# One accumulating DMA issued behind two sums of w1 instead of ahead of them, in a gated MLP kernel

## The chip, the core and the metric

The kernel runs on one core of a Trainium2 chip. The core has five engines that run side by side, each with its own queue in program order: TensorE (PE, matrix products), VectorE (DVE), ScalarE (ACT), GpSimd (POOL) and SyncE (SP). DMAs are issued from the queues of SyncE, GpSimd and ScalarE and all share the core's 16 DMA engines. An engine waits on semaphores for the data of others; whatever stands behind a waiting instruction on the same engine waits too. The metric is the time on the device in microseconds (us).

## What is computed

```python
# x (16, 256, 512), w1 (512, 4096), w2 (2048, 512), float32
h = x @ w1
gate, value = np.split(h, 2, axis=-1)
h = np.maximum(gate, 0) * value
return (h @ w2).astype(np.float32)
```

With the first two axes of x joined there are 4096 rows.

## The kernel before

The rows are worked in four sets of 1024 (`SET`, loop over `s`). Both products use a scheme of the Strassen and Winograd kind: operands are split in two by two, and seven products (P1 to P7) of sums of the parts stand in for eight. So each operand needs sums besides its own parts: T1 to T4 of the weights (`TURNS`), S1 to S4 of x and of g (`SUMS`). All operands are float16, sums on TensorE's side are kept in PSUM in float32.

**First product.** The hidden dimension is cut in 16 blocks `jb` of 128. A block takes seven slots of two matmuls of 128x512 (`Block`, L195 on, matmuls at L202). In the loop P1, P5, P2, P6 and P3, P7, P4 of neighbouring blocks are interleaved (`SLOT`, `PERIOD`). In set 0, blocks 0 to 3 are done in the ordinary way (`Plain`). ScalarE and VectorE turn the results into g = relu(gate) * value (L209 to L241); g is written as float16.

**Second product.** `mm2_stream` (matmuls at L286, 128x256) yields one matmul at a time. It starts while the last blocks of the first product end, and its last `TAIL` steps run into the next set. Its operands are w2's parts, the sums of w2 and the sums of g (L275). In set 0 the order of its steps is P1 and P2 for three row blocks, then P5, P6, P3, P7, P4: P5 needs T1 and S1, P6 needs T2 and S2, P3 needs S4, P7 needs T3 and S3, P4 needs T4.

**Weights.** w1 comes in six chunks (`CHUNKS`), cast to float16 by GpSimd's DMAs (L352). Its sums T1 to T4 are made on GpSimd, one chunk after the other (L160, `w1_one`), each reading what the two parts hold or what an earlier sum has made: T1 from B12 and B11, T2 from B22 and T1, T3 from B22 and B12, T4 from B21 and T2, all added. The last chunk (blocks 12 to 15) is one instruction of 128x1024 for each T. The sums of w2 are made by DMAs alone: SyncE copies parts of w2 to where T1, T2 with T3, and T4 will be (L536), then GpSimd issues accumulating DMAs, which add a source to what stands at the destination (L163, `add_w2`). T3 and T2 are the two halves of one tile, `v_12`, which one copy fills; the profile calls its tile `v`, and the tiles of T1 and T4 `v_T`. The T3 add needs that copy. The T2 add reads T1, so it needs the T1 add to have landed. The T4 add reads T2.

**x.** `cast_x(1)` (L359, a DMA of GpSimd) writes set 1 of x to DRAM as float16. SyncE reads it back transposed (L388). VectorE makes its sums (L451).

**What sets the order.** The scheduling is manual: each engine runs its instructions in the order in which the program text emits them. On GpSimd, around the change, that is: w1 sums of chunks 1 to 4; the T1 and T2 sums of the last chunk (start 40.30 and 42.50); the T1 add of w2 (44.57); the T3 add (50.08); the T3 and T4 sums of the last chunk (50.66, 52.75); the T2 add (54.81); the cast of x (55.39); four sums of g, two for S1 and two for S3 (from 55.95); the T4 add (64.28); one more sum of g for S1 (64.90). VectorE then makes the remaining sums of g of set 0 (L574 to L579): a quarter of S1 (128x1024), S2 in two halves, S4 in two halves, half of S3.

Of the kernel before, what the change touches and what calls it, by code (L numbers as in the profile page):

```python
# [29 lines left out]
@with_exitstack  # L30
def kernel(ctx: ExitStack, tc: tile.TileContext, x, w1, w2, out):

    nc = tc.nc
    x2 = x.flatten_outer_dims()
    out2 = out.flatten_outer_dims()  # L40
    flagpool = ctx.enter_context(tc.tile_pool(name="flagpool", bufs=1))
    flag = flagpool.tile([1, 1], dt.int32, name="flag")
    with ExitStack() as fast:
        unfit = fast_way(fast, tc, x2, w1, w2, out2, flag)
    with tc.If(unfit > 0, label="general"):
        with ExitStack() as general:
            general_way(general, tc, x2, w1, w2, out2)
# [52 lines left out]
def fast_way(ctx, tc, x2, w1, w2, out2, flag):  # L100
# [54 lines left out]
    def w1_ops(eng, jb, n):  # L155
        for t in TURNS:
            w1_one(eng, jb, n, *t)

    def w1_one(eng, jb, n, m, a, b, o):
        eng.tensor_tensor(W(m, jb, n), W(a, jb, n), W(b, jb, n), op=o)  # L160

    def add_w2(m, v):
        nc.gpsimd.dma_start(out=V[m], in_=V[v], accum_op=ADD)  # L163
# [12 lines left out]
    def x_tiles():  # L176
        o = {f"A{h}": xpool.tile([P, 4, TH], F16, name=f"x_A{h}") for h in (1, 2)}
        for h in (1, 2):
            for k in (1, 2):
                o[f"A{h}{k}"] = o[f"A{h}"][:, 2 * k - 2:2 * k]  # L180
        for n in ("S1", "S2", "S3", "S4"):
            o[n] = xpool.tile([P, 2, TH], F16, name=f"x_{n}")
        return o
# [88 lines left out]
    def g_sum(eng, go, n, h0, h1):  # L272
        for m, i0, i1, op in SUMS:
            if m == n:
                eng.tensor_tensor(go[n][:, h0:h1], go[i0][:, h0:h1], go[i1][:, h0:h1], op=op)  # L275
# [69 lines left out]
    def advance(stream, n):  # L345
        for _ in range(n):
            if stream is None or next(stream, 0) == 0:
                return
# [5 lines left out]
    def fetch_w2(i):  # L354
        ks, n = slice(i // 2 * NHC, i // 2 * NHC + NHC), i % 2
        nc.gpsimd.dma_start(out=w2_h[n][:, ks], in_=w2_v[:, ks, n * HALF:(n + 1) * HALF])  # L356

    def cast_x(s):
        nc.gpsimd.dma_start(out=x16[s], in_=x2[s * SET:(s + 1) * SET, :])  # L359

    def g_tiles():
        g = gpool.tile([P, NJ, SET], F16, name="g")
        gs = {n: gpool.tile([P, NHC, TH], F16, name=f"g_{n}") for n in ("S1", "S2", "S3", "S4")}
        return g, g_ops(g, gs)
# [21 lines left out]
    def turn_by_dma(s, o, h):  # L386
        for k in range(2):
            nc.sync.dma_start_transpose(out=o[f"A{h + 1}{k + 1}"], in_=x16[s][h * TH:(h + 1) * TH, k * 256:k * 256 + 256])  # L388
# [7 lines left out]
    def fetch_rows(s, q):  # L396
        rows[s, q] = xpool.tile([P, 2, D], F16, name=f"xn{q % 2}")
        nc.sync.dma_start(out=rows[s, q], in_=x16[s][q * 256:(q + 1) * 256].rearrange("(b p) d -> p b d", p=P))
# [50 lines left out]
    def x_sum(o):  # L449
        n, i0, i1, op = sums.pop(0)  # L450
        nc.vector.tensor_tensor(o[n], o[i0], o[i1], op=op)  # L451
# [64 lines left out]
    for s in range(NS):  # L516
        if s:
            g, go = g_tiles()
        first = NPLAIN if s == 0 else 0
        blocks = {jb: Block(xo, g, jb) for jb in range(first, NJ)}  # L520
        if s == 0:
            blocks[first] = lead
        plan = {jb * PERIOD + at: (jb, n) for jb in blocks for n, at in SLOT.items() if (s, jb, n) != (0, first, "P1")}
        last = NJ * PERIOD
        stream = mm2_stream(s, go)
        if s == 0:
            w1_ops(nc.gpsimd, 4, 2)
            fetch_w2(0)
            fetch_w2(1)
            w1_ops(nc.gpsimd, 6, 2)  # L530
            fetch_w2(2)
            fetch_w2(3)
            w1_ops(nc.gpsimd, 8, 2)
            w1_ops(nc.gpsimd, 10, 2)
            for to, v in ((V["T1"], V["B11"]), (v_12, w2_h[1]), (V["T4"], V["B21"])):
                nc.sync.dma_start(out=to, in_=v)  # L536
            for t in TURNS:
                w1_one(nc.gpsimd, 12, 4, *t)
                if t[0] == "T2":
                    add_w2("T1", "B12")  # L540
                    add_w2("T3", "B22")
            add_w2("T2", "T1")
            cast_x(1)
        for at in range(first * PERIOD, last + PERIOD):
            if at in plan:
                jb, n = plan[at]
                if n == "P1" and s and jb in (4, 8):
                    fetch_rows(s, 1 + jb // 4)
                if n == "P2" and s == 0 and jb in (11, 13, 15):
                    h = jb - 11  # L550
                    if h == 4:
                        add_w2("T4", "T2")
                    for m in ("S1", "S3")[:2 - h // 4]:
                        g_sum(nc.gpsimd, go, m, h, h + 2)
                getattr(blocks[jb], n)()
                ended = jb - (n == "P7") if n == "P7" or (n, jb) == ("P4", NJ - 1) else -1
                if ended in blocks:
                    blocks[ended].finish()
                if n == "P5":
                    for f in LOOKS.get((s, jb), ()):  # L560
                        f()
                if ended >= 0 and s:
                    if ended < NHC:
                        g_sum(nc.gpsimd, go, "S3", ended, ended + 1)
                        if s == 1 and ended in (1, 4):
                            cast_x(2 + ended // 4)
                    elif ended < NJ - BY_DVE:
                        for m in ("S1", "S2", "S4"):
                            g_sum(nc.gpsimd, go, m, ended - NHC, ended - NHC + 1)
            elif at >= last:  # L570
                advance(stream, 4)
            else:
                advance(prev, 4)
        if s == 0:  # L574
            g_sum(nc.vector, go, "S1", 6, 8)
            for m in ("S2", "S4"):
                for h in (0, NHC // 2):
                    g_sum(nc.vector, go, m, h, h + NHC // 2)
            g_sum(nc.vector, go, "S3", NHC // 2, NHC)  # L579
        else:  # L580
            for m in ("S1", "S2", "S4"):
                g_sum(nc.vector, go, m, NHC - BY_DVE, NHC)
        done = 20
        if s + 1 < NS:
            xo = x_tiles()
            for h in range(2):
                turn_by_dma(s + 1, xo, h)
            for q in range(2):
                fetch_rows(s + 1, q)
            advance(stream, 100)  # L590
            sums = list(SUMS)
            for _ in SUMS:
                x_sum(xo)
            if s == 0:
                w1_ops(nc.vector, 0, 2)
                w1_ops(nc.vector, 2, 2)
            advance(stream, MM2 - TAIL - 100 - done)
        else:
            advance(stream, MM2)
        prev = stream  # L600
# [29 lines left out]
```

## Time and profile before

| | us |
|---|---|
| median of 9 runs (lowest to highest) | 313.31 (311.46 to 313.77) |
| the profiled execution, its own time | 314.05 |
| its span, first to last instruction | 312.2 |
| TensorE matmul busy in the span | 302.1 |
| VectorE, ScalarE, GpSimd busy | 217.7, 188.7, 147.2 |
| mean granted TensorE clock | 0.996 |

The profile is of one execution. Busy times count matmuls up to modelled ends. A line of a timeline gives start, duration, engine, line of the kernel, operation, output and input tiles, shapes, and in brackets the engine's idle time in front of it and what ended that. A recorded start of a GpSimd instruction can lie ahead of the end of the one before it; ends follow one another. "DMA to landing" counts from the recorded start of the issue to the last byte's semaphore.

The stretch that the change touches runs from 44 to 74 us, where set 0 ends its first product and starts its second. The DMAs of w2's sums in it, by issue and landing:

| DMA | issued at | to landing |
|---|---|---|
| copy into T2 and T3 (`v_12`, 1024 KB), SyncE | 43.06 | 6.4 |
| T1 add (512 KB), GpSimd | 44.57 | 8.6 |
| T3 add (512 KB), GpSimd | 50.08 | 5.5 |
| T2 add (512 KB), GpSimd | 54.81 | 5.8 |
| cast of x, set 1 (1024 KB), GpSimd | 55.39 | 10.1 |
| T4 add (512 KB), GpSimd | 64.28 | 6.3 |

### The profile page before, as it was taken

To read this page: it belongs to the slowest core of one execution; us is meant where nothing else is said; L and a number is where in the kernel's file an instruction comes from. 1 tells how busy PE (TensorE), PEld (TensorE's weight loads), DVE (VectorE), ACT (ScalarE), POOL (GpSimd) and SP (SyncE) were. 2 spreads that over 40 slices of the span, in tenths; PEclk is the share of its full clock that TensorE was granted. 3 is DMA by queue.
4 is the path that set the end of the run, shared out by engine and by line. 5 is a ranking of instruction groups with operands and counts; after the bars stand their busy time and mean duration, and the time that the engine had idled before them with its cause. 6 is when DMAs were issued, how large, how long until landed. Compare 5 with 4: busy or idle time off the path is not lost.

```text
span 312.2 us, 5081 instructions
## 1 busy us (share of the span) xinstructions
PE 302.1 (97%) x1859; PEld 181.6 (58%) x1859; DVE 217.7 (70%) x330; ACT 188.7 (60%) x450; POOL 147.2 (47%) x135
## 2 busy tenths in 40 slices
PE   7999998998999999999999999999999999999993
PEld 4554443477864444468874444458885444448882
DVE  1377887898638888885428888886525888888311
ACT  3357765646766676748847676655857667673230
POOL 5779985970003346992001424995000434898000
PEclk9999999999999999999999999999999999999998
DMA  7999978969331770036321110028411101000113
GB/s 248 202 202 204 226 191 209 173 110 202 138 122 34 138 163 5 1 70 151 119 101 37 34 34 2 0 44 138 158 70 67 34 3 33 0 2 0 69 73 133
DMA packets 33449, 30.74 MB, mean 98 GB/s; under 512 B 13872, under 2 KB 27952, under 8 KB 33200
## 3 DMA queue, kind: packets, MB, share of 16 engines
q0 software_dynamic: 10704, 11.54, 22.9%
q1 hardware_dynamic: 22576, 18.75, 20.8%
q8 instruction: 15, 0.25, 0.3%
q10 hardware_dynamic: 144, 0.13, 0.1%
q14 instruction: 10, 0.08, 0.1%
HBM read 24.12 MB, written 11.53 MB: 114 GB/s over the span
## 4 chain that ended last, share of the span: by engine, by line
PE 78%; DMA 10%; POOL 6%; issue 2%; DVE 1%; ACT 0%; SPq 0%; DVEq 0%; POOLq 0%
PE Y L202 21%; PE X L202 14%; PE W L202 14%; PE Y L286 13%; PE W L286 8%; PE X L286 8%; DMA w<-in_w_dram 4%; POOL wt L160 4%; DMA wr<-in_w_dram 3%; DMA v<-w 2%; DVE g_S L275 1%; DMA g_S<-in_x_dram 1%; POOL w L356 1%; POOL wr L352 1%; POOL g_S L414 0%
## 5 line engine op out<-in xcount | busy, mean ns | idle before, releaser
L275 POOL TENSOR_TENSOR g_S<-g 128x512 f16<-128x512 f16 (+1 forms) x47 | 60.5, 1331 | 126.0 <-DVE g L241 124.0
L202 PEld LDWEIGHTS <-wt 128*128 128x128 f16 x480 | 46.8, 98 | 57.1 <-POOL wt L160 2.3
L202 PE MATMUL Y<-x_S,wt 128*128 128x512 f16 x240 | 71.4, 379 | 1.1 <-POOL wt L160 1.1
L202 PE MATMUL X<-x_A,wr 128*128 128x512 f16 x240 | 71.4, 379 | 0.0
L202 PEld LDWEIGHTS <-wr 128*128 128x128 f16 x360 | 35.2, 98 | 40.7 <-issue 0.2
L229 DVE SCALAR_TENSOR_TENSOR cc<-W,pu 128x512 f32<-128x512 f32 x60 | 41.5, 692 | 23.6 <-ACT pu L223 23.6
L209 ACT COPY Y<-X 128x512 f32<-128x512 f32 x60 | 34.2, 571 | 37.8 <-PE X L202 37.4
L286 PEld LDWEIGHTS <-g_S 128*128 128x128 f16 x512 | 49.7, 98 | 7.5 <-DVE g_S L275 1.6
L235 DVE SCALAR_TENSOR_TENSOR cc<-Y,pu 128x512 f32<-128x512 f32 x60 | 41.5, 692 | 7.9 <-PE Y L202 2.0
L223 ACT ACTIVATE pu<-Y 128x512 f32<-128x512 f32 x60 | 35.8, 597 | 15.6 <-PE Y L202 15.6
L230 DVE SCALAR_TENSOR_TENSOR g<-X,cc 128x512 f16<-128x512 f32 x60 | 41.5, 692 | 2.3
L286 PEld LDWEIGHTS <-g 128*128 128x128 f16 x384 | 37.6, 98 | 8.2
L241 DVE SCALAR_TENSOR_TENSOR g<-Y,cc 128x512 f16<-128x512 f32 x60 | 40.9, 682 | 1.8 <-PE Y L202 1.8
L216 ACT ACTIVATE pu<-W 128x512 f32<-128x512 f32 x60 | 36.2, 603 | 0.3 <-PE W L202 0.3
L202 PE MATMUL Y<-x_A,wt 128*128 128x512 f16 x120 | 35.7, 379 | 0.3 <-POOL wt L160 0.2
L202 PE MATMUL W<-x_S,wr 128*128 128x512 f16 x120 | 35.7, 379 | 0.0
L202 PE MATMUL W<-x_S,wt 128*128 128x512 f16 x120 | 35.7, 379 | 0.0
L286 PE MATMUL Y<-v,g_S 128*128 128x256 f16 x256 | 30.8, 273 | 0.5 <-DVE g_S L275 0.5
L286 PE MATMUL X<-w,g 128*128 128x256 f16 x256 | 31.2, 273 | 0.0
L316 DVE SCALAR_TENSOR_TENSOR o<-W,pv 128x256 f32<-128x256 f32 x16 | 6.8, 424 | 30.2 <-PE W L286 30.2
L275 POOL TENSOR_TENSOR g_S<-g,g_S 128x512 f16<-128x512 f16 x18 | 21.8, 1209 | 1.4
L275 POOL TENSOR_TENSOR g_S<-g_S,g 128x512 f16<-128x512 f16 x18 | 20.8, 1155 | 1.4
(69 smaller groups left out, 296.1 us busy)
## 6 DMA issues: line engine op xcount, KB each, us to landing
out_dram<-o SPq DMA_DIRECT2D x16, 256.0 KB, 2.0
out_dram<-pv SPq DMA_DIRECT2D x15, 256.0 KB, 2.0
x<-in_x_dram POOLq DMA_DIRECT2D x3, 1024.0 KB, 8.1
xn<-x SPq DMA_DIRECT2D x12, 256.0 KB, 3.2
wr<-in_w_dram POOLq DMA_DIRECT2D x4, 512.0 KB, 14.3
w<-in_w_dram POOLq DMA_DIRECT2D x4, 512.0 KB, 11.8
wr<-in_w_dram POOLq DMA_DIRECT2D x6, 256.0 KB, 8.8
g_S<-in_x_dram SPq DMA_DIRECT2D x2, 512.0 KB, 4.8
```

The source lines that it names most:

```text
L160: eng.tensor_tensor(W(m, jb, n), W(a, jb, n), W(b, jb, n), op=o)
L202: nc.tensor.matmul(ps, W(wn, self.jb)[:, b], self.xo[xn][:, b, :], start=fresh and b == 0, stop=b == 1, skip_group_check=True)
L209: nc.scalar.copy(out=self.Y, in_=self.X)
L216: nc.scalar.activation(self.p5, self.W, COPY, scale=GS)
L223: nc.scalar.activation(self.u2, self.Y, COPY, scale=-GS)
L229: nc.vector.scalar_tensor_tensor(out=self.c12, in0=self.W, scalar=GS, in1=self.u2, op0=MULT, op1=ADD)
L230: nc.vector.scalar_tensor_tensor(out=self.g[:, self.jb, :TH], in0=self.X, scalar=0.0, in1=self.c12, op0=MAX, op1=MULT)
L235: nc.vector.scalar_tensor_tensor(out=self.c22, in0=self.Y, scalar=-GS, in1=self.p5, op0=MULT, op1=ADD)
L241: nc.vector.scalar_tensor_tensor(out=self.g[:, self.jb, TH:], in0=self.Y, scalar=0.0, in1=self.c22, op0=MAX, op1=MULT)
L275: eng.tensor_tensor(go[n][:, h0:h1], go[i0][:, h0:h1], go[i1][:, h0:h1], op=op)
L286: nc.tensor.matmul(ps, go[gn][:, k, b * P:(b + 1) * P], V[vn][:, k, :], start=fresh and k == 0, stop=k == NHC - 1, skip_group_check=True)
L316: nc.vector.scalar_tensor_tensor(out=d["o1"][:, HALF:], in0=d["W"], scalar=1 / GS, in1=d["pu"][:, 1], op0=MULT, op1=ADD)
```

## The change

The T3 add moves from inside the loop over the sums of the last chunk to behind the loop:

```diff
             for t in TURNS:
                 w1_one(nc.gpsimd, 12, 4, *t)
                 if t[0] == "T2":
                     add_w2("T1", "B12")
-                    add_w2("T3", "B22")
+            add_w2("T3", "B22")
             add_w2("T2", "T1")
             cast_x(1)
```

GpSimd's order becomes: T1 and T2 sums of w1, T1 add, T3 and T4 sums of w1, T3 add, T2 add, cast of x. Compared instruction by instruction, GpSimd's queue differs in this one move, with the same waits on each instruction; the queues of the other four engines are the same.

## The prediction, made before the changed kernel ran

> **What bounds the kernel now.** I read the page first: TensorE is busy for 97% of the span, so only its holes can be won, and the hidden engines matter only where it waits for them:
>
> ```profile
> PE 302.1 (97%) x1859; PEld 181.6 (58%) x1859; DVE 217.7 (70%) x330; ACT 188.7 (60%) x450; POOL 147.2 (47%) x135
> ```
>
> Next the waits of TensorE, its holes with a known releaser:
>
> ```profile
> PE Y L202 <- POOL wt L160: 1.3, 2, 1.1
> PE Y L174 <- DVE warm L167: 1.3, 1, 1.3
> PE X L259 <- ACT x_A L377: 1.2, 2, 0.7
> PE Y L286 <- DVE g_S L275: 0.5, 1, 0.5
> PE W L286 <- DVE g_S L275: 0.4, 1, 0.4
> ```
>
> Columns: who waits, for whom, total us, times, longest. The first row is TensorE waiting for GpSimd's w1 sums; rows four and five are waits for the sums of g before the second product of set 0. The timeline of GpSimd shows why the w1 sums are late:
>
> ```profile
> 44.57 0.94 POOL L163 DMA_DIRECT2D v_T<-w  x1
> 50.08 0.88 POOL L163 DMA_DIRECT2D v<-w  x1 [4.57 <-DMA v<-w]
> 50.66 2.45 POOL L160 TENSOR_TENSOR wt<-wr 128x1024 f16<-128x1024 f16 x1
> 52.75 2.44 POOL L160 TENSOR_TENSOR wt<-wr,wt 128x1024 f16<-128x1024 f16 x1
> 54.81 1.20 POOL L163 DMA_DIRECT2D v<-v_T  x1
> 55.39 1.16 POOL L359 DMA_DIRECT2D x<-in_x_dram  x1
> ```
>
> [...]The first DMA adds into T1, the second into T3. The second waits 4.57 us for the copy of w2 into v_12 (SyncE, issued 43.06, landed 49.50), and the two sums of w1, which need nothing of it, stand behind it. Last, TensorE in that place:
>
> ```profile
> 51.43 0.59 PE L202 MATMUL W<-x_S,wt 128*128 128x512 f16 x2
> 53.16 0.60 PE L202 MATMUL Y<-x_S,wt 128*128 128x512 f16 x2 [1.14 <-POOL wt L160]
> ...
> 54.47 0.59 PE L202 MATMUL W<-x_S,wr 128*128 128x512 f16 x2
> 55.24 0.39 PE L202 MATMUL Y<-x_A,wt 128*128 128x512 f16 x1 [0.18 <-POOL wt L160]
> ```
>
> A pair of matmuls starts every 0.43 us in steady state. 51.43 to 53.16 is 1.73, so 1.30 too long; 54.47 to 55.24 is 0.77, 0.34 too long. The full hole is **1.64 us**, from starts (the idle notes, 1.14 and 0.18, count from modelled ends).
>
> **The change, part by part.** One DMA instruction of GpSimd moves past two sums; nothing is added or removed, and the orders of TensorE, VectorE, ScalarE and SyncE stay. The order of GpSimd's DMAs (T1, T3, T2, cast of x) stays too.
>
> *The two sums.* They follow the T1 add, which ends at 45.51. By ends, one takes 2.1 us (53.11 less 50.96; 55.19 less 53.11). They end near 47.7 and 49.8. TensorE wants them at 51.9 and 54.5, less what it has gained: over 2 us to spare. The 1.64 us hole goes. What runs beside them is VectorE's L229 to L241, which already ran beside GpSimd's earlier sums at the same 2.12 us.
>
> *The T3 add.* The copy lands at 49.50 as before; by then the sums are done (49.8 at worst, overlapping the 0.55 us from landing to start), so it runs 50.08 to 50.96 as before. Cost nothing; the sums now fill its wait. If the copy landed 0.5 us sooner, the sums would be the later party, still at no cost to TensorE.
>
> *A new wait: the T2 add.* It reads T1, so it waits for the T1 add to land, 8.6 us after its issue: 44.57 + 8.6 = 53.17. Before, the sums covered this. Now GpSimd is free at 50.96 and stands 2.2 us there, with the cast of x, four g sums, the T4 add and the fifth g sum queued behind. From landing to start took 0.55 us on the T3 add, so T2 starts at 53.74, ends at 54.62 (0.88, the T3 row), the cast at 55.16 (0.54 by ends). Before, the cast ended at 56.55. GpSimd's queue is **1.39 us** early by ends; by starts (53.74 against 54.81) 1.07. I take the ends, since a start is recorded while its forerunner still runs; 1.07 is kept as the low end.
>
> Here a rule and a row differ. The row: 8.6 us for this 512 KB add. The Trainium skill, "DMA: Bandwidth & Descriptors", section "Anatomy of one DMA", gives about 2.0 us plus bytes over 436 GB/s, as an estimate 3.2 us for 512 KB: T1 would land at 47.8 and no new wait exist. Then GpSimd would stand over 4 us early and the g sums no longer hold anything: a gain near 2.9 us (worked out below). The trace's four accumulating DMAs took 5.5 to 8.6 us, so I take the row.
>
> *The sums of g.* After TensorE's last first-product matmul, the chain is GpSimd's fifth sum, then VectorE's sums, up to TensorE's matmuls at 73.10 (timelines of GpSimd and of VectorE):
>
> ```profile
> 64.28 1.51 POOL L163 DMA_DIRECT2D v_T<-v  x1
> 64.90 3.04 POOL L275 TENSOR_TENSOR g_S<-g 128x1024 f16<-128x1024 f16 x1
> ```
>
> ```profile
> 64.97 0.69 DVE L241 SCALAR_TENSOR_TENSOR g<-Y,cc 128x512 f16<-128x512 f32 x1 [0.45 <-PE Y L202]
> 65.70 2.80 DVE L275 TENSOR_TENSOR g_S<-g 128x1024 f16<-128x1024 f16 x1
> 68.42 2.35 DVE L275 TENSOR_TENSOR g_S<-g_S,g 128x2048 f16<-128x2048 f16 x2
> 70.69 2.35 DVE L275 TENSOR_TENSOR g_S<-g,g_S 128x2048 f16<-128x2048 f16 x2
> ```
>
> VectorE's 128x1024 sum takes 2.80 us here, though one of 128x2048 takes 1.2: it stands until GpSimd's sum ends (67.94) and is done 0.56 later. TensorE's starts between 67.83 and 73.10 are 1.33 us longer than its pitch (0.11, 0.70, 0.51): a second hole, released by VectorE. So TensorE, 1.64 early, meets a chain that is early by another amount, and the chain decides.
>
> GpSimd's fifth sum ends at 67.94 - 1.39 = 66.55 (its g rows come with TensorE, 1.6 us early, in time). VectorE's sum is ready at 65.70 - 1.64 = 64.06. The Trainium skill, "SBUF — State Buffer", section "Who interferes with whom": a VectorE operation with two SBUF inputs and a GpSimd operation that reads SBUF exclude each other for a whole instruction, by order of issue. The 2.80 row agrees on exclusion. On order the row leaves it open: VectorE started at 65.70, between GpSimd's recorded start (64.90) and the end of the DMA instruction in front (65.79), and lost. If GpSimd is first again: 66.55 + 0.56 + four sums of 1.135 = 71.66, against 73.04: **1.38 gained**. If VectorE goes first at 64.06, it is done by 64.65, GpSimd's sum runs to 66.80, and 66.80 + 4.54 = 71.34: **1.70 gained**. I take the middle, **1.5 us**.
>
> *Behind it.* From 73.10 TensorE has no wait left, so it carries the gain to the end. The cast of x landed 10.1 us after issue and released SyncE's transposes at 65.58; both come 1.1 to 1.4 us earlier. If the last transpose is late by some tenths, VectorE's x sums at 76.71 take it, and VectorE has 1.92 us idle before 84.30. More casts and adds overlap for 1 us; the adds of T2 and T4 have over 5 us of slack.
>
> Sum: span 312.2 - 1.5 = 310.7; the profiled execution 314.05 - 1.5 = 312.55. The runs shown have a median of 313.31, 0.74 below that execution; from it **311.8 us**.
>
> **Rivals.**
> - *Nothing binds at the g sums* (0.08): T1 lands soon after 50, or the chain reorders well. TensorE keeps 1.64 + 1.33 = 2.97, say 2.9: 310.4. Against: the 8.6 us row.
> - *Mostly given back at the g sums* (0.14): GpSimd's queue is early by only 0.5 us, because T1 lands 0.9 later (its transfer shares the DMA engines with the copies) or a sum meets VectorE. The 1.64 turns into a longer hole at 73: 312.8. For: this chain already ends last there. Against: no traffic of the T1 add changes before it lands. That the change misses its aim is this case as well, with nothing left.
> - *Slower* (0.07): the new wait for T1's landing. Zero gain is where T1 lands at 53.17 + 1.39 = 54.56, 10.0 us after issue; every later us costs one, through cast, g sums and the hole at 73. Others of GpSimd's DMAs took up to 12.7 us (w2's loads); at that T1 lands at 57.3, the loss is 2.7, the time 316.0. For: two sums now run right behind its issue. Against: the T3 add had two sums behind it and landed in 5.5.
> - *The forecast*, gain 1.0 to 2.0: 0.71, 311.3 to 312.3.
>
> **How the numbers follow.** A change under 0.3% (0.94 us) can't be told from none. Faster: nearly all of the forecast (0.69 of 0.71) and the first rival (0.08): 0.77. Within: 0.02 and the second rival's 0.14: 0.16. Slower: 0.07. The range runs from part of the way to the first rival (a gain of 2.4, 310.9) to the second (a gain of 0.4, 312.9). Left out: most of the slower case, half of the first rival, and what the scatter of the runs (311.46 to 313.77) does to a median.
>
> **What would show it.** Right: no idle before the two L160 sums, which start near 45.2; no TensorE wait for wt; the T3 add still near 50.1; a GpSimd wait of about 2.5 us before the T2 add, at 53.7; the fifth g sum ending near 66.5; the last VectorE g sum at 71.3 to 71.7; TensorE's waits for g_S grown, not gone. Wrong: T1's landing past 54.5, or the copy of w2 landing elsewhere than 49.5.

## The result and the profile after

The changed kernel takes **311.71 us** (median of 10 runs, 311.27 to 312.15); the kernel before takes 313.39 us (31 runs, 311.46 to 313.83). The ratio is 0.9952, 95% interval [0.9939, 0.9966]. That is 1.68 us less; 1.5 us had been forecast (311.8 us). The profiled execution of the changed kernel has a time of 311.67 us and a span of 309.8 us, so it lies at its median. The one shown of the kernel before lay 0.7 us above its own. The two spans therefore differ by 2.4 us, which is more than the kernels do. Seven of the 22 executions of `g_first` (below) were in a slow state, with granted clocks of 0.987 to 0.992 and 317.8 to 320.8 us, and are left out of its figures; no other kernel here had one.

The waits of TensorE after the change (who waits, for whom, total us, times, longest):

```profile
PE Y L174 <- DVE warm L167: 1.3, 1, 1.3
PE X L259 <- DVE wr L392: 0.7, 1, 0.7
PE W L286 <- DVE g_S L275: 0.4, 1, 0.4
PE X L259 <- ACT x_A L377: 0.3, 1, 0.3
PE X L259 <- ACT x_A L384: 0.3, 1, 0.3
```

The row for GpSimd's `wt` is gone. Of the two rows for `g_S` one is left. (The other rows are of the first 19 us of the kernel.) In TensorE's timeline the pair of matmuls that had started at 53.16, 1.73 us behind the one in front, now follows at the pitch of 0.43:

```profile
51.46 0.59 PE L202 MATMUL W<-x_S,wt 128*128 128x512 f16 x2
51.89 0.59 PE L202 MATMUL Y<-x_S,wt 128*128 128x512 f16 x2
```

The timeline of GpSimd in the same place:

```profile
44.80 0.94 POOL L163 DMA_DIRECT2D v_T<-w  x1
45.46 2.45 POOL L160 TENSOR_TENSOR wt<-wr 128x1024 f16<-128x1024 f16 x1
47.55 2.43 POOL L160 TENSOR_TENSOR wt<-wr,wt 128x1024 f16<-128x1024 f16 x1
49.62 1.21 POOL L163 DMA_DIRECT2D v<-w  x1
52.84 0.85 POOL L163 DMA_DIRECT2D v<-v_T  x1 [2.01 <-DMA v_T<-w]
53.38 0.85 POOL L359 DMA_DIRECT2D x<-in_x_dram  x1
...
62.25 1.19 POOL L163 DMA_DIRECT2D v_T<-v  x1
62.87 2.73 POOL L275 TENSOR_TENSOR g_S<-g 128x1024 f16<-128x1024 f16 x1
```

The two sums now fill the time in which GpSimd stood for the copy. The T3 add issues as early as before; the copy landed at 48.99, ahead of the end of the sums (49.98), so it has no wait of its own left. The new wait is there: 2.01 us before the T2 add, for the T1 add to land. VectorE's sums of g behind GpSimd's last one:

```profile
64.06 2.10 DVE L275 TENSOR_TENSOR g_S<-g 128x1024 f16<-128x1024 f16 x1
66.09 2.35 DVE L275 TENSOR_TENSOR g_S<-g_S,g 128x2048 f16<-128x2048 f16 x2
68.36 2.35 DVE L275 TENSOR_TENSOR g_S<-g,g_S 128x2048 f16<-128x2048 f16 x2
```

The first still takes 2.10 us, against 2.80: it again stands until GpSimd's sum ends (62.87 + 2.73 = 65.60), and 0.56 us later it is done. The last of these ends at 70.71. TensorE needs it for the second half of the first P3 step of the second product, before and after the change:

```profile
73.10 1.48 PE L286 MATMUL W<-w,g_S 128*128 128x256 f16 x12 [0.35 <-DVE g_S L275]
70.77 1.48 PE L286 MATMUL W<-w,g_S 128*128 128x256 f16 x12 [0.35 <-DVE g_S L275]
```

To compare executions I take three starts of TensorE from each trace: A, the pair of matmuls in front of the first hole (51.43 in the kernel before), B, the last pair of the first product (64.34), and C, the second half of that P3 step (73.10). Without a hole B - A is 11.27 and C - B is 7.43. What exceeds that is hole 1 (for the sums of w1) and hole 2 (for the sums of g). "Last g sum" is the end of GpSimd's fifth sum of g. All are us. Where a kernel ran several times the time is the median; the other columns are of its one profiled execution.

| execution | time | T3 add starts | T1 lands | T2 add starts | last g sum | A | hole 1 | hole 2 |
|---|---|---|---|---|---|---|---|---|
| before, as shown | 313.39 | 50.08 | 53.13 | 54.81 | 67.94 | 51.43 | 1.64 | 1.32 |
| changed | 311.71 | 49.62 | 52.55 | 52.84 | 65.61 | 51.46 | 0 | 0.63 |
| `after_again` | 311.66 | 49.65 | 52.55 | 52.84 | 65.63 | 51.21 | 0 | 0.89 |
| `before_again` | 313.27 | 49.79 | 52.80 | 54.53 | 67.65 | 51.36 | 1.42 | 1.33 |
| `before_again2` | 313.03 | 49.65 | 52.70 | 54.40 | 67.51 | 51.49 | 1.14 | 1.33 |
| `late_copy_before` | 312.97 | 49.24 | 51.03 | 53.98 | 67.09 | 51.32 | 0.91 | 1.32 |
| `late_copy_after` | 311.07 | 50.12 | 51.92 | 52.22 | 64.98 | 51.91 | 0 | 0 |
| `split_copy` | 311.25 | 45.43 | 51.58 | 51.87 | 64.69 | 51.74 | 0 | 0 |
| `t1_early` | 311.01 | 50.31 | 45.40 | 50.92 | 64.02 | 51.38 | 0 | 0 |
| `t1_late` | 312.35 | 49.68 | 53.71 | 54.00 | 66.76 | 51.95 | 0 | 1.29 |
| `pad1` | 311.62 | 49.78 | 52.83 | 53.11 | 65.92 | 51.38 | 0 | 1.02 |
| `pad2` | 313.40 | 49.71 | 52.73 | 54.50 | 67.60 | 51.20 | 0 | 2.89 |
| `g_first` | 313.98 | 49.72 | 53.17 | 55.05 | 67.84 | 51.95 | 0 | 1.76 |
| `g_first_cast` | 310.91 | 50.83 | 52.92 | 55.62 | 65.01 | 51.60 | 0 | 0 |

Two regularities carry the whole reading. In the four executions in which the two sums of w1 stand behind the waiting T3 add, hole 1 is the start of the T3 add, less A, plus 2.98 or 2.99 us, in each of them: the hole moves with that DMA one for one. And wherever hole 2 is left, in either order, C follows the last g sum by 5.15 or 5.16 us, `g_first` alone excepted (4.55: VectorE's first sum was done there, at 65.25, before GpSimd's last one began, and only four sums were left). From 73 or 70 us on TensorE has no wait in either trace: C to the end is 239.07 us before and 239.02 after, so the gain is made by then and kept. (Among all executions here that stretch scatters from 238.56 to 239.45, without a wait of TensorE; an agreement to 0.05 is closer than that.)

### The profile page after: what moved, and what is told of

Same layout as the page of the kernel before. It is cut to its first block, busy times and chain, and to the rows that moved or that the text cites. A ratio compares the mean times of both kernels' runs of the same rounds, so it can differ in the third digit from the quotient of the medians.

```text
span 309.8 us, 5081 instructions
## 1 busy us (share of the span) xinstructions
PE 301.8 (97%) x1859; PEld 182.1 (59%) x1859; DVE 217.2 (70%) x330; ACT 188.8 (61%) x450; POOL 147.2 (48%) x135
## 4 chain that ended last, share of the span: by engine, by line
PE 91%; DVE 2%; DMA 2%; ACT 1%; issue 1%; SPq 0%; DVEq 0%
PE Y L202 25%; PE X L202 16%; PE W L202 16%; PE Y L286 13%; PE W L286 8%; PE X L286 8%; PE X L259 2%; PE W L259 2%; DMA g<-in_w_dram 2%; DVE g_S L275 1%; ACT v L264 0%; ACT x_A L384 0%; DVE cc L229 0%; DVE g L241 0%; DVE x_A L377 0%
## 5 line engine op out<-in xcount | busy, mean ns | idle before, releaser
L202 PEld LDWEIGHTS <-wr 128*128 128x128 f16 x360 | 35.2, 98 | 40.7 <-issue 0.2
```

The source lines that it names most:

```text
L202: nc.tensor.matmul(ps, W(wn, self.jb)[:, b], self.xo[xn][:, b, :], start=fresh and b == 0, stop=b == 1, skip_group_check=True)
```

## The experiments

### The changed kernel again

> The changed kernel once more, as the measure for the other runs on this chip. Theory (two holes of TensorE: the wait for the w1 sums near 53 us is gone, the one for the g sums near 70 us is halved because GpSimd's queue waits for the T1 add to land): 311.7 us, T1 landed near 52.6, TensorE held for g_S by about 0.65 us. Rival (the execution profiled after the change was a lucky one): the second hole is back at 1.3 us or more and the time nearer 312.5.

Measured: 311.66 us, ratio to the kernel before 0.9953 [0.9937, 0.9968]; T1 landed at 52.55, hole 2 is 0.89 us. As the theory has it. The hole differs from the first execution by 0.26 because TensorE came 0.25 us sooner to A while GpSimd came at the same time.

### The old order without its wait

```diff
-            for to, v in ((V["T1"], V["B11"]), (v_12, w2_h[1]), (V["T4"], V["B21"])):
+            for to, v in ((V["T1"], V["B11"]), (V["T3"], V["B12"]), (V["T2"], V["B22"]), (V["T4"], V["B21"])):
                 nc.sync.dma_start(out=to, in_=v)
```

> The order of before, with the copy of w2 into v_12 cut in two, so that the half for T3 is issued some 9 us sooner. Theory (the old order costs only because the T3 add waits for that copy): no wait before the T3 add, the two w1 sums done near 50.3, no TensorE wait for wt, then the same wait for T1's landing: 311.7 us, as the changed kernel. Rival (the place of the T3 add matters by itself, its descriptors or its traffic holding up the sums or the T1 add): well above, 312.6 to 313.4.

Measured: 311.25 us, 0.9939 [0.9922, 0.9956]. The copy for T3 now lands at 42.74, and the T3 add no longer waits:

```profile
44.79 0.94 POOL L163 DMA_DIRECT2D v_T<-w  x1
45.43 1.21 POOL L163 DMA_DIRECT2D v<-w  x1
46.02 2.77 POOL L160 TENSOR_TENSOR wt<-wr 128x1024 f16<-128x1024 f16 x1
48.10 2.77 POOL L160 TENSOR_TENSOR wt<-wr,wt 128x1024 f16<-128x1024 f16 x1
51.87 0.86 POOL L163 DMA_DIRECT2D v<-v_T  x1 [1.00 <-DMA v_T<-w]
```

This is GpSimd's timeline of that kernel, in the order of before, without the 4.57 us. So the place of the T3 add costs TensorE nothing by itself; what cost was its wait. It even came out 0.4 us below the forecast, as T1 landed at 51.58, a microsecond sooner than in the changed kernel, and hole 2 went too. Half of the copy into `v_12` had been moved by then; that this left less traffic beside the T1 add is the likely reason, but was not tried by itself.

### The T1 add sooner

```diff
+            add_w2("T1", "B12")
             for t in TURNS:
                 w1_one(nc.gpsimd, 12, 4, *t)
-                if t[0] == "T2":
-                    add_w2("T1", "B12")
             add_w2("T3", "B22")
```

> The changed kernel with the T1 add issued one step sooner, ahead of the last chunk's T1 and T2 sums, so that it lands near 48 to 50. Theory (T1's landing holds GpSimd by 2.0 us and through it the g sums): no wait before the T2 add, the fifth g sum ends near 63.6, ahead of VectorE's at 64.06, and the second hole of 0.65 us goes: 311.05 us. Rival (the g sums wait for g's rows or for VectorE, not for T1): 311.7, the hole stays.

Measured: 311.01 us, 0.9931 [0.9913, 0.9948], 0.65 us below the changed kernel on the same chip; 311.05 was expected. T1 lands at 45.40, 5.07 us after its issue, which was 2.6 us ahead of the copies (40.33 and 42.96). VectorE's first sum (its timeline in this kernel) is free of GpSimd:

```profile
63.99 0.69 DVE L275 TENSOR_TENSOR g_S<-g 128x1024 f16<-128x1024 f16 x1
64.60 2.35 DVE L275 TENSOR_TENSOR g_S<-g_S,g 128x2048 f16<-128x2048 f16 x2
```

0.69 us in place of 2.10, since GpSimd's last sum had ended at 64.02. Hole 2 is gone. So T1's landing, through GpSimd's queue, was what held the rest of the gain.

### Useless work in the new wait

```diff
             add_w2("T3", "B22")
+            nc.gpsimd.tensor_tensor(go["S3"][:, 4:6], W("T3", 12, 4), W("T4", 12, 4), op=ADD)
             add_w2("T2", "T1")
```

> The changed kernel with one useless sum of 128x1024 (2.15 us) on GpSimd between the T3 add and the T2 add; it writes into a part of S3 that VectorE overwrites later. Theory (GpSimd stands there for 2.0 us for T1's landing): the sum fills the wait, the queue is 0.1 to 0.3 us later, 311.8 us. Rival (GpSimd's own work, not T1's landing, sets the g sums): 2.1 us later, 313.8.

Measured: 311.62 us, 0.9957 [0.9940, 0.9973]: no dearer than the changed kernel. GpSimd's timeline:

```profile
50.42 2.42 POOL L542 TENSOR_TENSOR g_S<-wt 128x1024 f16<-128x1024 f16 x1
53.11 0.86 POOL L163 DMA_DIRECT2D v<-v_T  x1 [0.28 <-DMA v_T<-w]
```

A whole sum went in, up to T1's landing (52.83), and a last 0.28 us of the wait is still left. A second one, in the same place (`for h in (4, 6)`):

> The changed kernel with two useless sums of 128x1024 on GpSimd between the T3 add and the T2 add. One of them filled the wait for T1 (0.28 us of it was left). Theory: the second has no cover, so the T2 add and all behind it are 2.1 less 0.28, 1.9 us, later than with one, and TensorE's hole at the g sums grows by that: 313.5 us, T2 add near 55.0, the fifth g sum ending near 67.8. Rival (slack behind the T2 add): 311.6 to 312.5.

Measured: 313.40 us, 1.0016 [0.9995, 1.0037]. The second costs 1.78 us by the medians (the two ran on different chips); 1.9 was expected. Hole 2 grows from 1.02 to 2.89. This is the price of the prediction's slower case: once the cover is used up, time ahead of the T2 add is time of the kernel, here nearly one for one.

### The T1 add later

```diff
-                if t[0] == "T2":
-                    add_w2("T1", "B12")
+            add_w2("T1", "B12")
             add_w2("T3", "B22")
```

> The changed kernel with the T1 add too behind the T3 and T4 sums of w1, so that it is issued near 49.7 instead of 44.8. This is the slower case of the prediction made on purpose: T1 lands near 55.2 to 57.4, the T2 add starts 2.6 to 4.9 us later than 52.84, everything behind it too. Theory: one for one through the g sums, 314.3 to 316.5, the wait shown at TensorE for g_S, none for wt. Rival (slack behind the T2 add takes some of it): under 313.

Measured: 312.35 us, 0.9973 [0.9962, 0.9984]: by its ratio a little slower than the changed kernel (the two intervals just overlap), but far less than expected; the number is the rival's. GpSimd's timeline:

```profile
54.00 0.85 POOL L163 DMA_DIRECT2D v<-v_T  x1 [3.12 <-DMA v_T<-w]
```

The mechanism held: the T2 add, the last g sum and C all come 1.15 to 1.16 us later than in the changed kernel, and C follows the last g sum by 5.16; no slack took anything. The size didn't: issued 4.25 us later, T1 landed only 1.16 us later. At 49.05 one of the copies had just landed (49.01), the other did at 50.22, and the add took 4.66 us instead of 7.75. The expectation had reckoned with 5.5 to 7.8.

### The T2 add behind two sums of g

```diff
-            add_w2("T2", "T1")
             cast_x(1)
...
                         g_sum(nc.gpsimd, go, m, h, h + 2)
+                    if h == 0:
+                        add_w2("T2", "T1")
```

> The changed kernel with the T2 add issued behind the first two g sums of GpSimd, so that these fill the wait for T1. Theory: no wait before the T2 add, the T4 add then waits for T2 near 61.5 to 62.3, the fifth g sum ends near 64.6 (65.6 before), the second hole shrinks from 0.65 to 0.1 us or less: 311.1 us. Rival (the hole is set by VectorE's chain behind its own operands, not by GpSimd): 311.7.

Measured: 313.98 us, 1.0031 [1.0011, 1.0052]. Slower than the kernel before, against the expectation. GpSimd's timeline:

```profile
50.33 1.15 POOL L359 DMA_DIRECT2D x<-in_x_dram  x1
50.88 4.83 POOL L275 TENSOR_TENSOR g_S<-g 128x1024 f16<-128x1024 f16 x2
55.05 1.50 POOL L163 DMA_DIRECT2D v<-v_T  x1
55.67 5.11 POOL L275 TENSOR_TENSOR g_S<-g 128x1024 f16<-128x1024 f16 x2
64.81 0.87 POOL L163 DMA_DIRECT2D v_T<-v  x1 [4.03 <-DMA v<-v_T]
```

The wait ahead of the T2 add is filled, but the T4 add, which reads T2, now waits 4.03 us: T2 landed 9.48 us after its issue (5.49 in the changed kernel). The cast of x, 1 MB, had been issued ahead of it and landed at 62.04. One wait was traded for a longer one. Of the profiled execution (313.48 us) this explains the second hole, 1.76 us. The 15 runs lie between 312.30 and 316.73, twice as wide as those of the kernel before; one profile doesn't tell what the longer runs do. Moving the cast behind the T2 add tests the cause:

```diff
-            add_w2("T2", "T1")
-            cast_x(1)
...
+                    if h == 0:
+                        add_w2("T2", "T1")
+                        cast_x(1)
```

> The run that put the T2 add behind two g sums was slower since its T2 add took 9.5 us to land and the T4 add waited 4.0 us for it. There the cast of x had been issued 5 us ahead of it. Here the cast goes behind the T2 add. Theory (the cast's traffic ahead of the T2 add made it slow): T2 lands in 5.5 to 6 us, before the T4 add wants it, no wait there, the fifth g sum ends near 63.6, no hole: 311.0 us, unless the cast, 3 us later than in the changed kernel, makes VectorE's sums of x late (then up to 313). Rival (T2 is slow in that place whatever stands ahead): the T4 add waits again, 313 or more.

Measured: **310.91 us**, 0.9925 [0.9909, 0.9942], the lowest of all medians here, though not to be told from `t1_early`; both beat the changed kernel. T2 lands after 6.07 us, at 61.69, just as the sums end (61.88), and the T4 add waits no more than 0.10 us. So it was the cast ahead of the T2 add that made it slow. The last g sum ended at 65.01, not 63.6, as in this execution GpSimd was 1.2 us later from the start of the last chunk on. The late cast does show, in VectorE's timeline, and costs nothing, since VectorE has the time:

```profile
76.03 0.69 DVE L451 TENSOR_TENSOR x_S<-x_A 128x1024 f16<-128x1024 f16 x1 [2.08 <-DMA x_A<-x]
```

### The copy of w2 later, in both orders

```diff
-            for to, v in ((V["T1"], V["B11"]), (v_12, w2_h[1]), (V["T4"], V["B21"])):
+            for to, v in ((V["T1"], V["B11"]), (V["T4"], V["B21"]), (v_12, w2_h[1])):
```

> The kernel before with SyncE's copy into v_12 issued behind the copy for T4 instead of ahead of it; it should land about 1.2 us later (near 50.7). Theory: the T3 add, the two w1 sums and TensorE's first hole move with it one for one, 314.4 us. Rival (the stall is hidden behind the g sums anyway): 313.3, no change.

> The changed kernel with the same late copy into v_12. Theory: the sums of w1 don't stand behind the copy any more, and the T3 add has until T1's landing (52.6) at no cost; the T4 copy, now first, shares the DMA engines as before: 311.7 us, at most 0.5 more. Rival (the new order still hangs on this copy): 1 us more, 312.7.

Measured: 312.97 us, 1.0004 [0.9991, 1.0018], and 311.07 us, 0.9929 [0.9913, 0.9946]. The edit failed to do what it was made for. The T4 copy needs a part of w2 that is there sooner, so it went out at 39.7 to 40.7 instead of near 43.6. The copy into `v_12` still went out when its own part was there (42.38 in the old order) and took 6.30 us there, about as ever (6.0 to 6.4 in the three executions of the kernel before); it landed at 48.67, not near 50.7. With that the first says nothing on a later copy. In its profile the T3 add is early and hole 1 small (0.91), on the line of the other executions; its median doesn't show a gain from it. In the new order T1 lands at 51.92 and hole 2 goes, as in `split_copy` and `t1_early`: 0.6 us below what was expected.

### The kernel before, twice more

> The kernel before, one more profiled execution. Its runs lie between 311.5 and 313.9, those of the changed kernel between 311.3 and 312.3. Theory (the old order's time follows the landing of the copy into v_12): the start of the T3 add (50.08 in the execution shown) differs, and the span differs from 312.2 by as much as the two holes of TensorE (1.64 and 1.33 us there) differ. Rival (scatter from elsewhere, the clock or the start): same T3 add and holes, another span.

> The same as the run before it, a third execution of the kernel before, with the same expectations: the span goes with the start of the T3 add and the two holes, or by the rival it doesn't.

Measured: 313.27 and 313.03 us, spans 311.4 and 311.2 against 312.2. The T3 add starts at 49.79 and 49.65, and hole 1 shrinks with it by 0.22 and 0.50; hole 2 stays, since GpSimd's queue and TensorE both follow the T3 add there. That is about a quarter and a half of what the spans differ by. The rest lies behind C (238.58 us in both, 239.07 in the one shown), with no wait of TensorE. So the scatter of the old kernel comes in part from that copy's landing and in part from elsewhere, which stays open.

## Why the prediction came out right, step by step

- **Hole 1 goes, 1.64 us.** Right: the sums started at 45.46 and ended at 49.98 (49.8 forecast), and the hole is zero in all executions with the new order. (TensorE's want of the second sum, given as 54.5, is 54.47 + 0.43 = 54.90 by the lines shown; the slack was larger still.)
- **The T3 add costs nothing.** Right: it ended at 50.83, 50.96 before; `split_copy` shows that its place is indifferent to TensorE. The copy landed at 48.99, which the prediction had named as a sign of being wrong ("elsewhere than 49.5"); the sums were then the later party, and that cost nothing, as the prediction had said for this case.
- **A new wait for T1's landing.** Right in kind, too large in size: 2.01 us, where the prediction's own figures make it 2.78 (53.74 less 50.96; its "about 2.5" doesn't follow from them). This is the term that was mis-sized: "GpSimd's queue is 1.39 us early by ends" measured 2.33 (the last g sum at 65.61 against 67.94). 0.62 us of the difference is T1's landing, 52.55 and not 53.17: 8.6 us had been taken from one execution, and it was the longest: the eight with SyncE's copies as they were and the T1 add issued by 44.9 range from 7.7 to 8.6. Another 0.28 us is the step from landing to start, taken from the T3 add's wait (0.57) and measured at 0.29 on this one. So one sign failed: TensorE's waits for `g_S` were to have grown. A gain of 1.5 with TensorE 1.64 early would have made hole 2 about 1.47 us; it shrank from 1.33 to 0.63.
- **The fit of the Trainium skill** ("DMA: Bandwidth & Descriptors", "Anatomy of one DMA"), 3.2 us as an estimate for 512 KB, was rightly left aside: these adds took 4.66 us at the least and up to 10.78 among others' traffic (the T4 add of `g_first`).
- **The chain through VectorE.** Right: GpSimd was first, which was the 1.38 us branch of the two that the prediction averaged, and C is the last g sum plus 5.16, the sum that the prediction used (0.56 and four times 1.135, and 0.06 to the matmul). Its other branch, VectorE first, didn't occur in the changed kernel; in `g_first` it did, as GpSimd was waiting for T2. On who goes first, recorded starts stay no guide: there VectorE's next sum, started at 65.17, stood until GpSimd's sum, started at 65.43, had ended (67.84).
- **Nothing is lost behind it.** Right: no wait of TensorE behind C, and a stretch of the same length within its scatter.

Put together on the execution shown, the steps should have given 2.3 us, not 1.5: of the 2.96 us of both holes 0.63 is left. The median moved by 1.68, because that execution of the kernel before had larger holes than its usual one: in the two others the holes sum to 2.75 and 2.47, and 0.63 to 0.89 left of them is a gain of 1.6 to 2.1. So part of the closeness of 311.8 to 311.71 is luck: two errors offset each other, a term of 0.9 us too pessimistic and a profile on the slow side of its kernel. The range held both.

The rival in which nothing binds at the g sums lies, on the execution shown, about as near to what happened as the forecast does: 2.33 us of the 2.96 were kept. Where the wait for T1 was shortened or filled and both holes went, the medians are 310.91 to 311.25, not 310.4, since that number was reckoned from the larger holes of the execution shown. The rival in which the gain goes back there had the wrong sign: T1 landed 0.62 us sooner, not 0.9 later. The slower rival was priced about right (`pad2`) but far from deciding: even T1's add issued 4.25 us later moved its landing by 1.16. Its "up to 12.7 us" for other DMAs of GpSimd left out the longest: w1's loads (L352) took up to 16.1 in the same trace.

## What to carry to other kernels

An instruction that waits for a transfer belongs behind work on its queue that doesn't need it, and the place is free as long as what is fed by the waiting instruction has slack: here the sums ended 1.0 us after the copy had landed, and nothing was lost. Having moved it, look for the next wait on the same queue: here the landing of a DMA that had been covered became the limit, and issuing that DMA one step sooner gave another 0.65 us. When a transfer is moved, ask what else is under way at its new time and what was issued ahead of it; among the executions here an accumulating DMA of 512 KB took from 4.66 to 10.78 us.

## What the runs showed of the hardware beyond this

- The T1 add, an accumulating DMA of 512 KB, landed 4.66 us after its issue when one of SyncE's copies was through and the other nearly so, 5.07 when issued 2.6 us ahead of them, 6.9 to 8.6 when issued 1.3 to 2.2 us behind the first of them; the T2 add took 9.48 behind a cast of 1 MB and 6.07 ahead of it.
- From landing to the recorded start of the waiting DMA instruction on GpSimd took 0.56 to 0.57 us where SyncE's copy was awaited and 0.28 to 0.30 where GpSimd's own add was, in every execution with such a wait. The number of semaphores doesn't explain it: the T3 add names two and took 0.57, the T2 add of `split_copy` names two as well and took 0.29. The cause was not tried.
- A recorded start of a GpSimd instruction lay up to 0.96 us ahead of its forerunner's end. Ends were the sounder measure: the last g sum ended 2.33 us earlier after the change, the T2 add's end moved by 2.32 and its recorded start by 1.97; a sum of 128x1024 took 2.1 to 2.2 us by ends.
